# Seven block products for eight in a SwiGLU's gate and up projections, and the down projection moved behind all of them

## The chip, the cores and the metric

The kernel runs on one core of a Trainium2 chip. The metric is the time of one execution in microseconds (us) of the device. An engine's name is that of the profile: PE (TensorE, matmul), DVE (VectorE), ACT (ScalarE), POOL (GpSimd), SP (SyncE, which here issues every DMA).

## The reference

One layer of a hybrid decoder, for 1024 prompt tokens and 8 x 8 sampled ones: a mixer of attention and a state-space group, an output projection, and a SwiGLU feed-forward network (FFN), each between RMS norms. The change concerns the last lines.

```python
mix = jnp.concatenate([o_att.astype(x.dtype), o_ssm], axis=-1) @ w_out
x = x + rmsnorm(mix, g_post_mix)
f = rmsnorm(x, g_pre_ffn)
f = (jax.nn.silu(f @ w_gate) * (f @ w_up)) @ w_down
x = x + rmsnorm(f, g_post_ffn)
return x, new_k, new_v, new_conv, new_ssm
```

D_MODEL is 1024, D_FF is 2816 (22 tiles of 128), all in float32.

## The kernel before

The 1088 tokens stand in three chunks of 384, 384 and 320 columns, features on the partitions. Every float32 product is made of three products in the fp32r format: an operand x is split into xh (a rounding cast, on ACT) and xl = x - xh (on DVE or POOL), and a block of 128x128 weights costs the matmuls wh xh, wh xl and wl xh (`gemm`, L142 to L144). The weights come as raw lots of 128x512 (`load_w`, L119 to L126; 256 KB each): a DMA on SP, the cast on ACT at L125, the subtraction mostly on POOL at L126, with four raw buffers and five for each half.

The order on PE is written out by hand (`weave` gives PE filler work in gaps that the program names in us); on DVE, ACT, POOL and SP a scheduler sets it, and each engine runs its queue in that order.

When a chunk c has its mixer output, `chain(c)` (L1022) makes the norm behind the mixer (pm), the residual, and the norm ahead of the FFN (pf). A norm's sum of squares is added up by PE (`pm1st`), DVE makes the reciprocal root and a diagonal (`pm1d`), and PE broadcasts it (`pm1R`). For chunk 1 these names are pm1 and pf1, and what follows pf1R is f1: eight scalings (L1039), casts and subtractions. While chunk 2 goes through this, PE is filled by `first_up`: gate and up of the first three feature tiles over chunk 0, then 1.

The FFN then runs in eight groups of two or three feature tiles. `up_chunk` makes gate (og) and up (ou) of a tile and a chunk, and splits the result h into th and tl_, which stay in SBUF. Behind the tiles of a group, `down` makes the eight output tiles over the group's features alone and adds them to YP, at L1166 on DVE:

```python
for m in range(8):
    hi, lo = load_w(A["w_d"][m][:, ff0:ff0 + G, :], G, P, "wd%d_%d" % (gi, m))
    for c in range(3):
        down(m, [(hi[:, k, :], lo[:, k, :]) for k in range(G)], c)
```

The last group goes chunk by chunk, with the final norm `fin` (L1187, L1188) of a chunk beside the next one's products, and the outputs go out on SP.

Of the kernel before, what the change touches and what calls it, by code (L numbers as in the profile page):

```python
# [36 lines left out]
def hybrid_layer(ctx, tc, A):  # L37
# [1051 lines left out]
    with pool("chain") as kp:  # L1089

        th, tl_ = [], []

        def first_up():
            while "ch1" not in done:
                yield None
# [240 lines left out]
```

## Time and profile before

| | |
|---|---|
| time, median of 3 runs (lowest to highest) | 1747.24 us (1745.35 to 1752.21) |
| the profiled execution: time, span | 1751.08 us, 1749.3 us |
| mean granted clock of TensorE | 0.973 |
| busy in the span: PE, DVE, ACT, POOL | 1655.3, 881.5, 624.0, 631.4 us |
| DMA over the span | 171.13 MB, 98 GB/s |

Times in the rows are us from the span's start, of one execution. The busy time is a mean over stages: the mixer, up to about 900 us, where all engines work, and the FFN behind it, where PE is nearly always busy and the others are not. A row of the timeline gives start, length, engine, line and instruction (output <- inputs); in brackets stands the time in which its engine was idle just before it, and what ended that.

### The profile page before, as it was taken

The numbers are of one execution on the slowest core, as the hardware profiler recorded it, in microseconds if no ns is written. First come the engines' busy times: TensorE is split into PE (matmuls) and PEld (weight loads), VectorE is DVE, ScalarE is ACT, GpSimd is POOL, SyncE is SP. The second block draws the span as 40 slices with busy tenths as digits, with TensorE's granted clock in tenths as the row PEclk, the third lists the DMA queues.
The fourth block names the chain that finished last, engine by engine and source line by source line (L and its number), as shares of the span: only waits on it lengthen the run. The fifth ranks groups of instructions, "written<-read, shape, count | busy, mean of one in ns | idle before, by whom it ended". The sixth has DMA issues, their size and how long they took to land. (4 is left out here: it accounts for less than half of the span.)

```text
span 1749.3 us, 26692 instructions
## 1 busy us (share of the span) xinstructions
PE 1655.3 (95%) x9959; PEld 1560.4 (89%) x9959; DVE 881.5 (50%) x1917; ACT 624.0 (36%) x1397; POOL 631.4 (36%) x516
## 2 busy tenths in 40 slices
PE   8899999999799989899988999999999999999995
PEld 6899988887777877898988999999999999999995
DVE  6797667763588887346877401211212112121347
ACT  5242344431586676444543232112121121211221
POOL 5262356655554342223555222122222221221432
PEclk9899999999899999999989999999999999999997
DMA  5022564555553341543554111111111111110233
GB/s 185 25 79 99 155 177 141 163 171 194 149 150 93 93 145 58 175 128 105 175 176 143 39 49 41 44 47 38 50 42 50 41 41 46 41 57 22 82 103 102
DMA packets 146441, 171.13 MB, mean 98 GB/s; under 512 B 18120, under 2 KB 106696, under 8 KB 146280
## 3 DMA queue, kind: packets, MB, share of 16 engines
q1 hardware_dynamic: 146312, 169.43, 31.5%
q8 instruction: 78, 1.28, 0.3%
q14 instruction: 51, 0.42, 0.1%
HBM read 135.33 MB, written 36.28 MB: 98 GB/s over the span
## 5 line engine op out<-in xcount | busy, mean ns | idle before, releaser
L1055 DVE TENSOR_TENSOR sg<-sg,ou 128x384 f32<-128x384 f32 (+1 forms) x66 | 35.0, 532 | 393.3 <-PE ou L144 392.7
L1166 DVE TENSOR_TENSOR YP<-YP,od 128x384 f32<-128x384 f32 (+1 forms) x168 | 89.1, 532 | 126.2 <-PE od L144 126.0
L126 POOL TENSOR_TENSOR wg_1l<-wg_1r,wg_1h 128x512 fp32r<-128x512 f32 x20 | 25.9, 1294 | 211.6 <-ACT wg_1h L125 211.6
L1056 ACT CAST ffh<-sg 128x384 fp32r<-128x384 f32 (+1 forms) x66 | 32.6, 495 | 188.6 <-DVE sg L1055 188.3
L126 POOL TENSOR_TENSOR wi_1l<-wi_1r,wi_1h 128x512 fp32r<-128x512 f32 x40 | 56.1, 1403 | 73.9 <-ACT wi_1h L125 70.7
L1051 ACT ACTIVATE sg<-og 128x384 f32<-128x384 f32 (+1 forms) x66 | 31.1, 472 | 131.8 <-PE og L144 125.2
L126 POOL TENSOR_TENSOR wi_0l<-wi_0r,wi_0h 128x512 fp32r<-128x512 f32 x40 | 58.4, 1460 | 30.4 <-ACT wi_0h L125 27.5
L1057 DVE TENSOR_TENSOR ffl<-sg,ffh 128x384 fp32r<-128x384 f32 (+1 forms) x66 | 42.8, 650 | 33.9 <-ACT ffh L1056 33.8
L126 POOL TENSOR_TENSOR woa_1l<-woa_1r,woa_1h 128x512 fp32r<-128x512 f32 x24 | 33.7, 1405 | 64.8 <-ACT woa_1h L125 57.9
L126 POOL TENSOR_TENSOR wos_1l<-wos_1r,wos_1h 128x512 fp32r<-128x512 f32 x24 | 33.9, 1411 | 60.4 <-ACT wos_1h L125 54.8
L142 PE MATMUL ip<-x1h,wi_0h 128*128 128x384 f32 x128 | 48.4, 378 | 6.3 <-DVE cbuf L367 3.0
L380 DVE SCALAR_TENSOR_TENSOR cacc<-cbuf,vec,cacc 128x1112 f32<-128x1112 f32 x36 | 52.3, 1456 | 0.7
L142 PE MATMUL ip<-x0h,wi_0h 128*128 128x384 f32 x128 | 47.5, 371 | 4.5 <-DVE cbuf L367 3.6
L142 PE MATMUL ip<-x0h,wi_1h 128*128 128x384 f32 x128 | 45.6, 357 | 0.0
L144 PE MATMUL ip<-x0h,wi_0l 128*128 128x384 f32 x128 | 43.6, 341 | 1.5 <-POOL wi_0l L126 1.5
L142 PE MATMUL ip<-x1h,wi_1h 128*128 128x384 f32 x128 | 44.8, 350 | 0.0
L126 POOL TENSOR_TENSOR wd_1l<-wd_1r,wd_1h 128x384 fp32r<-128x384 f32 (+1 forms) x7 | 6.8, 973 | 105.2 <-ACT wd_1h L125 105.2
L144 PE MATMUL ip<-x1h,wi_0l 128*128 128x384 f32 x128 | 44.3, 346 | 0.0
L143 PE MATMUL ip<-x1l,wi_0h 128*128 128x384 f32 x128 | 44.2, 345 | 0.0
L143 PE MATMUL ip<-x0l,wi_0h 128*128 128x384 f32 x128 | 43.4, 339 | 0.4 <-DVE x0l L278 0.4
L126 POOL TENSOR_TENSOR wg_0l<-wg_0r,wg_0h 128x512 fp32r<-128x512 f32 x21 | 27.4, 1303 | 45.6 <-ACT wg_0h L125 45.6
L144 PE MATMUL ip<-x0h,wi_1l 128*128 128x384 f32 x128 | 43.8, 342 | 0.0
(840 smaller groups left out, 6136.3 us busy)
## 6 DMA issues: line engine op xcount, KB each, us to landing
wi_0r<-in_w_in SPq DMA_DIRECT2D x40, 256.0 KB
wi_1r<-in_w_in SPq DMA_DIRECT2D x40, 256.0 KB
wos_0r<-in_w_os SPq DMA_DIRECT2D x24, 256.0 KB
wos_1r<-in_w_os SPq DMA_DIRECT2D x24, 256.0 KB
woa_0r<-in_w_oa SPq DMA_DIRECT2D x24, 256.0 KB
woa_1r<-in_w_oa SPq DMA_DIRECT2D x24, 256.0 KB
wg_0r<-in_w_g SPq DMA_DIRECT2D x22, 256.0 KB
wg_1r<-in_w_g SPq DMA_DIRECT2D x22, 256.0 KB
```

What stands on the lines that cost most here:

```text
L126: (eng or g).tensor_sub(lo, raw, fr(hi))
L142: t.matmul(out, lhsT=wh, rhs=xh, start=k == 0, stop=False)
L143: t.matmul(out, lhsT=wh, rhs=xl, start=False, stop=False)
L144: t.matmul(out, lhsT=wl, rhs=xh, start=False, stop=k == n - 1)
L380: v.scalar_tensor_tensor(acc[:, :L], buf[:, k:k + L], vec[:, cw + k:cw + k + 1], acc[:, :L], ALU.mult, ALU.add)
L1051: s.activation(sg, og[:, :n], AF.Silu)
L1055: v.tensor_mul(sg, sg, ou[:, :n])
L1056: s.copy(hi[:, c0:c0 + n], sg)
L1057: v.tensor_sub(lo[:, c0:c0 + n], sg, fr(hi[:, c0:c0 + n]))
L1166: v.tensor_add(YP[m][:, c0:c0 + n], YP[m][:, c0:c0 + n], o[:, :n])
```

## The change

The gate and up projections of two feature tiles (2j and 2j+1) over the two chunks of 384 columns are taken as a product of 2x2 blocks: feature tiles by halves of D_MODEL, times halves of D_MODEL by chunks. In place of eight block products seven are made, by the Winograd form of Strassen's scheme. It needs four sums of weight blocks (S1 to S4, on DVE, for each pair and each of gate and up), four sums of the blocks of the two chunks (T1 to T4, made once in `chain(1)` on DVE and POOL and split into halves like every operand), and sums of the products, on DVE and POOL. B11 and B21 are chunk 0's halves, B22 the second half of chunk 1. A unit (`gu_unit`) is gate or up of one pair: 84 matmuls of 384 columns, and 48 of 320 for chunk 2, whose four block products are made as before. It splits eight lots of weights in place of four.

`first_up` runs the units of pairs 0 and 1 without chunk 2 while that chunk is in `chain(2)`; their chunk 2 part follows with the weights loaded again, and then pairs 2 to 10 whole. The products silu(gate) x up are written to DRAM (h_scr). When all are done, the down projection goes chunk by chunk: `h_load` fetches h in six lots of four feature tiles, two raw buffers (hs) for all, and splits them; then each output tile is made over all 22 feature tiles in one accumulation, its weights loaded for every chunk. `fin` of a chunk stands beside the next chunk's first tile, with four buffers for x2. The groups, YP and the last group's own arrangement go.

```diff
-FFG = [3, 3, 3, 3, 3, 3, 2, 2]
...
+    h_scr = dr.tile([P, NFF, TOK], F32, name="h_scr")
...
-    def chain(c, mt, acc, kp, F):
+
+    ops = {}
+
+    def hilo(name, hi, lo):
+        ops[name] = [(hi[:, k, :], lo[:, k, :]) for k in range(4)]
+
+    def chain(c, mt, acc, kp):
...
-        for k in range(8):
+
+        def scaled(k):
             v.scalar_tensor_tensor(mt[:, k, :], mt[:, k, :], vec[:, V_GPF + k:V_GPF + k + 1], R, ALU.mult, ALU.mult)
-            s.copy(F.hi(k), mt[:, k, :])
-            (g if k % 2 else v).tensor_sub(F.lo(k), mt[:, k, :], fr(F.hi(k)))
-
...
-    def up_chunk(ff, c, wg, wu, hi, lo):
...
+            return mt[:, k, :]
+
+        def split(h, l, k, x, e):
+            s.copy(h[:, k, :], x)
+            e.tensor_sub(l[:, k, :], x, fr(h[:, k, :]))
...
+        elif c == 1:
+
+            m0 = mix[0]
+            t1, t4, t3, t2 = m0[:, 0:4], m0[:, 4:8], mt[:, 0:4], mt[:, 4:8]
+            h, l = Half(c, "B22h"), Half(c, "B22l")
+            slots["B22"] = (h, l)
+            hilo("B22", h.t, l.t)
+            for k in range(4):
+                v.tensor_sub(t1[:, k, :], scaled(k), m0[:, k, :])
+            for k in range(4):
+                split(h.t, l.t, k, scaled(4 + k), g)
+                v.tensor_sub(t3[:, k, :], mt[:, 4 + k, :], mt[:, k, :])
+                v.tensor_sub(t2[:, k, :], mt[:, 4 + k, :], t1[:, k, :])
+                g.tensor_sub(t4[:, k, :], m0[:, 4 + k, :], t2[:, k, :])
+            while "op2" not in done:
+                yield 1.0
+            for name, x, e in (("T2", t2, v), ("T1", t1, v), ("T3", t3, g), ("T4", t4, g)):
+                h, l = Half(c, name + "h"), Half(c, name + "l", at=None if xfree else xl)
+                slots[name] = (h, l)
+                hilo(name, h.t, l.t)
+                for k in range(0, 4, 2):
+                    s.copy(h.t[:, k:k + 2, :], x[:, k:k + 2, :])
+                    e.tensor_sub(l.t[:, k:k + 2, :], x[:, k:k + 2, :], fr(h.t[:, k:k + 2, :]))
...
+    def prod(out, n, w, name, first=False):
+
+        for k in range(4):
+            (wh, wl), (xh, xl) = w[k], ops[name][k]
+            for i, (x, y) in enumerate(((wh, xh), (wh, xl), (wl, xh))):
+                t.matmul(out[:, :n], lhsT=x, rhs=y, start=first and k + i == 0, stop=k == 3 and i == 2,
+                         skip_group_check=not first)
...
+    def gu_unit(gp, src, j, up, sgs, wino, plain):
...
+        if wino:
+            pa, pb, pc = ps("mm", nm + "pa"), ps("s", nm + "pb"), ps("t", nm + "pc")
+            ssum(1, r[21], r[22], False)
+            ssum(2, S[1], r[11], True)
+        w = lot(r[11], 11)
+        if wino:
+            yield from prod(pa, n, w, "B11", True)
+            p1 = st("p1")
+            with tc.high_priority():
+                s.copy(p1, pa[:, :n])
+        if plain:
+            yield from prod(qa, n2, w, "F0", True)
+        if wino:
+            w = lot(S[2], "s2")
+            yield from prod(pb, n, w, "T2", True)
+            u2 = st("u2")
+            with tc.high_priority():
+                v.tensor_add(u2, p1, pb[:, :n])
+            w = lot(S[1], "s1", v)
+            yield from prod(pc, n, w, "T1", True)
+            p5 = st("p5")
+            with tc.high_priority():
+                s.copy(p5, pc[:, :n])
+            ssum(3, r[11], r[21], True)
+            ssum(4, r[12], S[2], True)
+        w = lot(r[12], 12)
+        if wino:
+            yield from prod(pa, n, w, "B21")
+            out(0, 0, 0, v, lambda dst: pa[:, :n])
+        if plain:
+            yield from prod(qa, n2, w, "F1")
+            out(4, 0, 2, v, lambda dst: qa[:, :n2])
+        if wino:
+            w = lot(S[3], "s3")
+            yield from prod(pb, n, w, "T3")
+            u3 = st("u3")
+            with tc.high_priority():
+                v.tensor_add(u3, p1, pb[:, :n])
+            out(1, 1, 1, g, add(g, u3, p5, u3))
+            w = lot(S[4], "s4", v)
+            yield from prod(pc, n, w, "B22")
+            out(2, 0, 1, g, add(v, u2, pc[:, :n], u2))
+        w = lot(r[22], 22)
+        if wino:
+            yield from prod(pb, n, w, "T4")
+            out(3, 1, 0, v, add(v, p1, pb[:, :n], p1))
+        if plain:
+            yield from prod(qb, n2, w, "F1", True)
+            w = lot(r[21], 21)
+            yield from prod(qb, n2, w, "F0")
+            out(5, 1, 2, v, lambda dst: qb[:, :n2])
...
+                while "ch2" not in done:
+                    yield from gu_pair(kp, part[0], plain=False)
+                    part[0] += 1
...
+            for j in range(part[0]):
+                run(gu_pair(gp, j, wino=False))
+            for j in range(part[0], NFF // 2):
+                run(gu_pair(gp, j))
...
+                x = dp.tile([P, 4, n], F32, tag="hs", bufs=2, name="hs%d_%d" % (c, i))
+                dma(x[:, :K], h_scr[:, q:q + K, c0:c0 + n])
+                s.copy(h[:, :K], x[:, :K])
+                v.tensor_sub(l[:, :K], x[:, :K], fr(h[:, :K]))
...
+                hi, lo = load_w(A["w_d"][m][:, q:q + K, :], K, P, "wd%d_%d" % (m, i), eng=v if i % 3 == 2 else g)
+                w = [(hi[:, k, :], lo[:, k, :]) for k in range(K)]
+                for k in range(K):
+                    (wh, wl), (xh, xl) = w[k], H[q + k]
+                    t.matmul(o[:, :n], lhsT=wh, rhs=xh, start=q + k == 0, stop=False)
+                    t.matmul(o[:, :n], lhsT=wh, rhs=xl, start=False, stop=False)
+                    t.matmul(o[:, :n], lhsT=wl, rhs=xh, start=False, stop=q + k == NFF - 1)
...
+            def x2_load(m):
+                x2 = dp.tile([P, n], F32, tag="x2", bufs=4, name="x2_%d" % m)
+                dma(x2, x2_scr[:, m, c0:c0 + n])
...
+        H = h_load(0, range(6), False)
+        for c, (c0, n) in enumerate(CH):
+            Y = dp.tile([P, 8, n], F32, tag="Y", bufs=2, name="Y%d" % c)
+            accs = [sp.tile([P, n], F32, tag="acc", bufs=2, name="acc")]
+            for m in range(8):
...
-            if not last:
-                for m in range(8):
-                    hi, lo = load_w(A["w_d"][m][:, ff0:ff0 + G, :], G, P, "wd%d_%d" % (gi, m))
-                    for c in range(3):
-                        down(m, [(hi[:, k, :], lo[:, k, :]) for k in range(G)], c)
```

On PE, what follows the broadcast pf1R in before is gate and up of tiles 0 and 1 over chunk 0 (f0h, f0l), 24 matmuls each, with chunk 2's norm (pm2st, pm2R) among them. The first use of f1 is the last row, 146 matmuls behind pf1R.

```order
L211 MATMUL pf1R_9718<-pf1d_9671,ones_76 128x128 x3
L142 MATMUL og0_0_9822<-f0h0_8558,wg0_0h_9760 128x384
L143 MATMUL og0_0_9822<-f0l0_8560,wg0_0h_9760 128x384
...
L142 MATMUL ou0_0_9849<-f0h0_8558,wu0_0h_9772 128x384
...
L197 MATMUL pm2st_9874<-ones_76,acc_8923 128x1 x3
L142 MATMUL og1_0_9901<-f0h0_8558,wg1_0h_9784 128x384
...
L142 MATMUL ou1_0_9928<-f0h0_8558,wu1_0h_9796 128x384
...
L211 MATMUL pm2R_9938<-pm2d_9894,ones_76 128x128 x3
...
L142 MATMUL og0_1_10079<-f1h0_9129,wg0_0h_9760 128x384
```

In the changed kernel there stand 12 products on B11 (of chunk 0), then the 12 on T2 and the 12 on T1, both made of chunk 1.

```order
L198 MATMUL pf1R_9718<-pf1d_9671,ones_76 128x128 x3
L1094 MATMUL g0pa_9790<-B11h_9105,g0w11h_9797 128x384
L1094 MATMUL g0pa_9790<-B11l_9106,g0w11h_9797 128x384
...
L1094 MATMUL g0pb_9791<-T2h_9758,g0ws2h_9815 128x384
...
L1094 MATMUL g0pc_9792<-T1h_9764,g0ws1h_9833 128x384
...
L1094 MATMUL g0pa_9790<-B21h_9119,g0w12h_9855 128x384
...
L184 MATMUL pm2st_9871<-ones_76,acc_8923 128x1 x3
L1094 MATMUL g0pb_9791<-T3h_9770,g0ws3h_9897 128x384
...
L1094 MATMUL g0pc_9792<-B22h_9724,g0ws4h_9918 128x384
...
L1094 MATMUL g0pb_9791<-T4h_9776,g0w22h_9937 128x384
...
L198 MATMUL pm2R_9947<-pm2d_9891,ones_76 128x128 x3
```

What moved: the first operand of chunk 1 is needed 12 matmuls behind pf1R, where it was 146, and chunk 2's pm2st stands behind the products on T2 and T1.

On DVE, this is what follows the diagonal pf1d in before: eight scalings of chunk 1 (tile mix1) and four subtractions.

```order
L205 TENSOR_SCALAR pf1d_9671<-cst_74,pf1y_9659 128x128 x3
L1039 SCALAR_TENSOR_TENSOR mix1_7919<-mix1_7919,vec_75,pf1R_9722 128x384
L1020 TENSOR_TENSOR acc_8923<-acc_8923,sq_9715 128x320
L1039 SCALAR_TENSOR_TENSOR mix1_7919<-mix1_7919,vec_75,pf1R_9722 128x384 x2
L1041 TENSOR_TENSOR f1l0_9131<-mix1_7919,f1h0_9129 128x384
L1039 SCALAR_TENSOR_TENSOR mix1_7919<-mix1_7919,vec_75,pf1R_9722 128x384 x3
L1041 TENSOR_TENSOR f1l0_9131<-mix1_7919,f1h0_9129 128x384
L1039 SCALAR_TENSOR_TENSOR mix1_7919<-mix1_7919,vec_75,pf1R_9722 128x384 x2
L1041 TENSOR_TENSOR f1l1_9132<-mix1_7919,f1h1_9130 128x384 x2
```

And in the changed kernel, where mix0 takes t1 and t4, mix1 the scaled chunk, t3 and t2; u0S are sums of up weights of pair 0, g0ws4l the lower half of a gate weight sum:

```order
L192 TENSOR_SCALAR pf1d_9671<-cst_74,pf1y_9659 128x128 x3
L1034 SCALAR_TENSOR_TENSOR mix1_7920<-mix1_7920,vec_75,pf1R_9722 128x384
L1008 TENSOR_TENSOR acc_8923<-acc_8923,sq_9715 128x320
L1113 TENSOR_TENSOR u0S1_10035<-u0r21_10026,u0r22_10028 128x512
L1056 TENSOR_TENSOR mix0_6626<-mix1_7920,mix0_6626 128x384
L1113 TENSOR_TENSOR u0S2_10037<-u0S1_10035,u0r11_10024 128x512
L1086 TENSOR_TENSOR g0ws4l_9919<-g0S4_9853,g0ws4h_9918 128x512
...
L1113 TENSOR_TENSOR u0S4_10095<-u0r12_10030,u0S2_10037 128x512
...
L1070 TENSOR_TENSOR T1l_9765<-mix0_6626,T1h_9764 128x768
...
L1070 TENSOR_TENSOR T2l_9759<-mix1_7920,T2h_9758 128x768
...
L1070 TENSOR_TENSOR T1l_9765<-mix0_6626,T1h_9764 128x768
L1070 TENSOR_TENSOR T2l_9759<-mix1_7920,T2h_9758 128x768
```

What moved: 30 operations stand from pf1R to the last T2l, the sums of chunks and of weights among them.

On SP, at the change from gate and up to down in the changed kernel; g10sg are the products of the last pair, hs0 the lots of h for chunk 0, wd1 the weights of the second output tile:

```order
L1134 DMA h_scr_91<-g10sg_14282 128x384
L1134 DMA h_scr_91<-g10sg_14296 128x320
...
L109 DMA wd1_1r_14762<-in_w_d 128x512
L1134 DMA h_scr_91<-g10sg_14385 128x320
L109 DMA wd1_2r_14780<-in_w_d 128x512
L1279 DMA hs0_0_14602<-h_scr_91 128x4x384
L1279 DMA hs0_1_14608<-h_scr_91 128x4x384
L1304 DMA x2_0_15564<-x2_scr_89 128x384
...
L1279 DMA hs0_2_14614<-h_scr_91 128x4x384
L1279 DMA hs0_3_14620<-h_scr_91 128x4x384
L109 DMA wd1_3r_14798<-in_w_d 128x512
...
L1279 DMA hs0_4_14626<-h_scr_91 128x4x384
```

What is new: the first load of h stands behind the last write of h, and four loads of x2 and some of weights stand among the loads of h.

## Rows read from the trace of the kernel before

**Rows 1.** Windows: stretch, length; busy us of each engine, granted clock, DMA share, GB/s.

```profile
900.00:920.00 20.00, 17.58 (x110) 16.96 (x108) 13.59 (x21) 9.45 (x19) 13.69 (x11) 0.91 0.69 201
920.00:940.00 20.00, 17.59 (x93) 17.11 (x93) 18.30 (x19) 9.20 (x20) 15.95 (x12) 0.91 0.47 148
...
1100.00:1200.00 100.00, 100.00 (x609) 100.00 (x608) 22.48 (x41) 18.97 (x36) 23.68 (x20) 1.00 0.15 46
...
1720.00:1735.00 15.00, 10.92 (x60) 10.20 (x60) 11.61 (x28) 4.20 (x9) 3.75 (x3) 0.78 0.37 133
```

**Rows 2.** Timeline of PE (start, length, instruction): 384-column products, first and thirteenth.

```profile
1149.78 0.35 PE L144 MATMUL og<-f0h,wg_0l 128*128 128x384 f32 x1
...
1151.88 0.34 PE L144 MATMUL og<-f0h,wg_1l 128*128 128x384 f32 x1
```

**Rows 3.** Timeline of PE: 320-column products, first and eighth of a run.

```profile
885.94 0.31 PE L142 MATMUL op<-sh,wos_0h 128*128 128x320 f32 x1
...
886.97 0.31 PE L143 MATMUL op<-sl,wos_0h 128*128 128x320 f32 x1
```

**Rows 4.** Timeline of PE after the first-chunk work, idle time and releaser in brackets.

```profile
921.68 0.46 PE L211 MATMUL pf1R<-pf1d,ones 128*128 128x128 f32 x2 [2.93 <-DVE pf1d L205]
...
943.52 1.62 PE L211 MATMUL pm2R<-pm2d,ones 128*128 128x128 f32 x6 [3.58 <-DVE pm2d L205]
```

**Rows 5.** Timeline of DVE round the broadcast pf1R.

```profile
924.58 0.62 DVE L1039 SCALAR_TENSOR_TENSOR mix<-mix,vec,pf1R 128x384 f32<-128x384 f32 x1 [1.63 <-ACT pf1R L218]
...
928.71 1.65 DVE L1041 TENSOR_TENSOR f1l<-mix,f1h 128x384 fp32r<-128x384 f32 x1
...
935.98 2.93 DVE L1039 SCALAR_TENSOR_TENSOR mix<-mix,vec,pf1R 128x384 f32<-128x384 f32 x2
...
941.05 0.56 DVE L1057 TENSOR_TENSOR ffl<-sg,ffh 128x384 fp32r<-128x384 f32 x1
```

**Rows 6.** Timeline of POOL, the first and last of seven back to back.

```profile
928.33 1.61 POOL L126 TENSOR_TENSOR wx<-wg_0r,wx 128x512 fp32r<-128x512 f32 x1
...
937.16 1.34 POOL L1041 TENSOR_TENSOR f1l<-mix,f1h 128x384 fp32r<-128x384 f32 x1
939.54 1.17 POOL L1041 TENSOR_TENSOR f1l<-mix,f1h 128x384 fp32r<-128x384 f32 x1 [1.04 <-ACT f1h L1040]
```

**Rows 7.** The instructions that read pf0R: min/median/max ns.

```profile
L1039 DVE SCALAR_TENSOR_TENSOR mix<-mix,vec,pf0R x8: 604/611/1646, 863.7 to 873.5; 128x384 f32<-128x384 f32 x8
```

**Rows 8.** Costliest groups (page) and DVE's groups by shape: busy, mean ns.

```profile
L126 POOL TENSOR_TENSOR wg_1l<-wg_1r,wg_1h 128x512 fp32r<-128x512 f32 x20 | 25.9, 1294 | 211.6 <-ACT wg_1h L125 211.6
...
L126 DVE TENSOR_TENSOR wos_0l<-wos_0r,wos_0h 128x512 fp32r<-128x512 f32 x24 | 17.6, 732 | 24.5 <-ACT wos_0h L125 21.7 <-issue 2.8
```

**Rows 9.** The instructions on tile gz: min/median/max ns.

```profile
L967 ACT ACTIVATE gz<-gz x6: 1271/1488/1492, 494.4 to 772.0; 128x1536 f32<-128x1536 f32 x4, 128x1280 f32<-128x1280 f32 x2
...
L968 POOL TENSOR_TENSOR gy<-gy,gz x6: 1557/2384/2620, 496.0 to 773.4; 128x768 f32<-128x768 f32 x4, 128x640 f32<-128x640 f32 x2
...
L971 DVE TENSOR_TENSOR gz<-gz x6: 806/952/959, 504.4 to 778.8; 128x768 f32<-128x768 f32 x4, 128x640 f32<-128x640 f32 x2
```

**Rows 10.** Timelines of SP (issues) and ACT (readers): 256 and 512 KB loads.

```profile
911.93 0.33 SPq L122 DMA_DIRECT2D wg_1r<-in_w_g  x1
...
914.81 0.62 ACT L125 CAST wg_1h<-wg_1r 128x512 fp32r<-128x512 f32 x1 [2.19 <-DMA wg_1r<-in_w_g]
...
277.55 0.36 SPq L540 DMA_DIRECT2D d_1ac<-ac_scr  x1
...
282.39 0.22 ACT L574 ACTIVATE d_1en<-d_1ac 128x8 f32<-128x8 f32 x1 [2.06 <-DMA d_1ac<-ac_scr]
```

**Rows 11.** Timeline of PE: the last group's end.

```profile
1721.18 0.42 PE L142 MATMUL od<-ffh,wx 128*128 128x320 f32 x1 [1.88 <-DVE sg L1055]
...
1724.78 0.39 PE L142 MATMUL od<-ffh,wx 128*128 128x320 f32 x1
...
1729.11 0.31 PE L144 MATMUL od<-ffh,wx 128*128 128x320 f32 x1
```

More of the change, by code (lines that the diff above doesn't have):

```diff
@@ new lines, in hybrid_layer, with split_w @@
+    slots, xl = {}, None
+    def split_w(raw, name, e):
+        hi = wp.tile([P, 4, P], F32R, tag="hi", bufs=5, name=name + "h")
+        lo = wp.tile([P, 4, P], F32R, tag="lo", bufs=5, name=name + "l")
+        s.copy(hi, raw)
+        e.tensor_sub(lo, raw, fr(hi))
+        return [(hi[:, k, :], lo[:, k, :]) for k in range(4)]
+    def prod(out, n, w, name, first=False):
+        for k in range(4):
+            (wh, wl), (xh, xl) = w[k], ops[name][k]
+            for i, (x, y) in enumerate(((wh, xh), (wh, xl), (wl, xh))):
+                t.matmul(out[:, :n], lhsT=x, rhs=y, start=first and k + i == 0, stop=k == 3 and i == 2,
+                         skip_group_check=not first)
+            if k == 1:
+                yield 6 * n / 2400.0
+        yield 6 * n / 2400.0
@@ L1059, in hybrid_layer, with gu_pair @@
+    def gu_pair(gp, j, wino=True, plain=True):
+        sgs = {}
+        for up in range(2):
+            yield from gu_unit(gp, A["w_u" if up else "w_g"], j, up, sgs, wino, plain)
     s_hl, o_hl, mix, acc = [None] * 3, [None] * 3, [None] * 3, [None] * 3
@@ L1074, in ch @@
             yield 1.0
-        fs.append(Split(c, "f%d" % c))
-        yield from chain(c, mix[c], acc[c], kp, fs[c])
+        yield from chain(c, mix[c], acc[c], kp)
         done.add("ch%d" % c)
@@ L1088, in hybrid_layer @@
     done.add("att2")
[L1089 to L1095, printed above, removed]
-            for j, x in (("h", th), ("l", tl_)):
-                x3 = fpool.tile([P, 3, TOK], F32R, tag="F", bufs=3, name="ff%s0" % j)
-                x.extend(x3[:, i, :] for i in range(3))
-            while "op2" not in done:
-                yield None
-            we = [Extra(kp, "s%s2_%d" % (j, q), 1, 2, CH[2][1]) for j in "hl" for q in range(2)]
-            w0 = [(load_w8(A["w_g"][i], P, "wg%d" % i, wq[0]), load_w8(A["w_u"][i], P, "wu%d" % i, wq[1]))
-                  for i, wq in enumerate(((None, None), ((None, kp), (kp, kp)), (we[:2], we[2:])))]
-            for c in range(3):
-                while "ch%d" % c not in done:
-                    yield None
-                for i in range(3):
-                    yield from up_chunk(i, c, w0[i][0], w0[i][1], th[i], tl_[i])
-        f = seq(f, lambda: op(2), first_up)
-        weave(seq(gate(2, kp), ch(0, kp), ch(1, kp), ch(2, kp)), f)
-        run(f)
@@ new lines, in hybrid_layer, with first_up @@
+    with pool("xl") as xl:
+        with pool("chain") as kp:
+            part = [0]
+            def first_up():
+                while "ch1" not in done:
+                    yield None
+                while "ch2" not in done:
+                    yield from gu_pair(kp, part[0], plain=False)
+                    part[0] += 1
+            f = seq(f, lambda: op(2), first_up)
+            weave(seq(gate(2, kp), ch(0, kp), ch(1, kp), ch(2, kp)), f)
+            run(f)
+        with pool("gu") as gp:
+            with tc.issue_after(wdma[0]):
+                for o, a in (("o_ks", "ck_nat"), ("o_vs", "cv_nat")):
+                    dma(A[o][:, 0:P - NT, :], A[a][:, NT:, :])
+            for j in range(part[0]):
+                run(gu_pair(gp, j, wino=False))
+            for j in range(part[0], NFF // 2):
+                run(gu_pair(gp, j))
```

224 lines of the change are left out of this document (107 added, 117 removed).

## The prediction

> **What bounds the kernel now.** I read the windows first. In the FFN TensorE (PE) is busy for the whole of 1100 to 1200 us at full clock, DVE and POOL for under a quarter of it [rows 1]: there time is a count of matmuls times their spacing, and helpers are free. It is otherwise at the seam where the FFN begins (900 to 940): PE is busy 17.6 of 20 us, DVE up to 18.3 and POOL up to 16.0 [rows 1]. There the question is which operand comes last. So I took PE's timeline for the spacing (2.10 us for 12 products of 384 columns, 0.174 each; 1.03 us for 7 of 320, 0.147 each) [rows 2, 3], and then its waits at the seam: 2.93 us for pf1R and 3.58 for pm2R, both on DVE [rows 4], and no wait of 0.4 us or more for the normed chunk f1 itself. That is because 146 matmuls (25 us) stand between pf1R and the first use of f1, as the order of before shows. The last place is the end: PE waits 1.88 us in the last group and then runs at half clock [rows 11].
>
> **What is removed on PE.** The FFN had 3168 products of 384 columns and 1584 of 320. Now a gate or up unit has 7 x 12 = 84 of 384 and 48 of 320, 22 units, and the down projection still has 1056 and 528. That is 2904 and 1584: 264 products fewer, all of 384 columns. 264 x 0.174 = **-46.0 us** [rows 2]. This needs PE to be the bound of each stage, which the rest is about.
>
> In the last group PE's stall goes too, since the up and down products are no longer alternated there: 1.88 us, and 12 products in 3.60 us where 0.147 each would be 1.76 [rows 3, 11]: **-3.7**.
>
> **pf1R, a little later.** Five DVE operations of 128x512 on weights now stand ahead of pf1d (g0S1, g0S2, g0S3, g0S4, g0ws1l). Alone they take 0.73 each [rows 8], 3.7 together, and 1.65 each, 8 together, at the pace of a DVE subtraction beside a busy POOL [rows 5]; a part of it fills waits that were there. **+3.5** (1.5 to 8).
>
> **The sums of chunk 1, the largest cost.** After pf1R the order now has only the 12 products on B11 (2.1 us), and then T2. T2 is a difference of a difference (t1 before t2), and the last to be split on DVE. On DVE 30 operations stand from pf1R to the last T2l: 8 scalings at 0.61 [rows 7], 12 sums of 384 columns at 0.56 [rows 5] and one of 320, 5 of 128x512 at 0.73 [rows 8], 4 of 768 columns at 0.95 [rows 9]: 19.5 us if nothing holds them. In the same stretch POOL has four B22l and four t4 at 1.17 [rows 6], and two of 768 columns, for which 1.9 is scaled from 1557 ns for 640 [rows 9]: 13.2 us. Do the two run beside each other? In before, POOL ran seven subtractions back to back from 928.33 to 938.50 [rows 6] (four of 512 columns at 1.29 alone, three of 384 at 1.17: 8.7 us), and DVE seven operations from 928.71 to 938.91 [rows 5] that alone take 5 x 0.61 + 2 x 0.56 = 4.2 us. So 12.9 us of work took 10.2: an overlap of 1.26, and a DVE scaling went from 0.61 to 1.4 or 1.6 [rows 5, 7]. By this 32.7 / 1.26 = 26 us, and some 2 us for ACT's casts and for u0S4, whose weight is asked for only behind u0S3 (2.9 us from issue to use) [rows 10]. T2 is there 28 us after pf1R, PE has 2.1 us to do: **+26** (18 with DVE's own 20 us; 32 if the two exclude each other, 32.7 us and 1 for a cast).
>
> By the Trainium skill (SBUF — State Buffer, section "SBUF: two separate sides") a DVE operation with two inputs in SBUF and a GpSimd operation that reads SBUF hold one port pair as an exclusive lock. The rows above agree that they slow each other, but the 1.26 says not all of it is serial; by the rule this term would be the upper one, +32.
>
> **Pairs 0 and 1 beside chunk 2.** 336 products of 384 columns, 58.5 us. POOL has 6 weight splits and 2 sums a unit, 6 x 1.29 + 2 x 1.17 = 10.1, 40 in four units, and some 12 of chunk 2; DVE's operations with both inputs in SBUF are near 23. 75 / 1.26 = 60 us, close to PE's 58.5, with pm2R and pf2R to wait for as before (3.58) [rows 4], and half clock behind a long wait as in [rows 11]. **+6** (1 to 12). In the plain part of these pairs that follows, a unit has 48 x 0.147 = 7.1 us of PE against 4 x 1.29 = 5.2 of POOL: **+1** (0 to 6). In the 18 full units PE has 21.7 us against 10 of POOL and about 9 of DVE, so nothing is added.
>
> **From gate and up to down.** Every lot of h now comes back from DRAM, and the load hs0_0 stands behind the last write of h on SP and waits for it. From the last up product: DVE's product 0.55, issue and write about 2.9 (as long as a 256 KB load takes to be used) [rows 10]; the load of 768 KB: 256 KB take 2.88 and 512 KB 4.84 from issue to reader [rows 10], so 6.8 by the same step; ACT's cast 1.5, and DVE's subtraction 1.75 from twice 0.95 [rows 9]. That is 13.5 us to the first lot, 12 if the write lands sooner. There are two buffers, so lots 2 and 3 wait for the subtraction of 0 and 1, and 4 and 5 for those of 2 and 3: about 10 us a turn. The sixth-but-one lot is split at 33 us, and 18 products follow it (3.1 us): the first output tile ends at 34 to 36 us instead of 66 x 0.174 = 11.5. **+22** (14 if loads take 4 us, at the 201 GB/s that one stretch of before shows [rows 1]; 27 if the weight loads of the same queue share it). Behind it a down tile needs 11.5 us of PE and 6 weight splits, 4 of them on POOL (5.2 us): PE bound again, and the changes of chunk, where the x2 loads and outputs queue on SP, **+2** (0 to 6).
>
> **The end.** Now as then some 20 us pass from the last product [rows 11] to the span's end at 1749.3. Four of the eight x2 tiles now load only when the output DMA of their buffer has ended: **+2** (1 to 4).
>
> **Sum.** -46.0 - 3.7 + 3.5 + 26 + 6 + 1 + 22 + 2 + 2 = +12.8. The profiled execution took 1751.08 us (1749.3 of span and 1.8 around it), 3.84 above the median: 1763.9, and 1760 beside the median of 1747.24.
>
> **Rivals.** Faster: DVE is not held by POOL at the seam. For it: the overlap comes from ten microseconds of one execution, with weight splits of POOL that stand elsewhere now. Against it: [rows 5] beside [rows 7]. pf1R costs 1.5 then, T2 18, pairs 0 and 1 1, the plain part 0; with a transition of 18 the sum is -46.0 - 3.7 + 1.5 + 18 + 1 + 18 + 2 + 1 = -8, or 1739, and lower if the loads are quicker too. It decides from the point where T2 is ready under about 22 us after pf1R. No gain and no loss: the first bubble is as computed, but the lots of h come in a stream and cost 10 instead of 22, because loads of one turn fly together and PE works on lots 0 to 3 meanwhile: +1, or 1748. For it speaks that the weights of the first tiles are already there; against it the two buffers. Much slower: POOL and DVE exclude each other. T2 at +32, pf1R +8, pairs 0 and 1 at 75 us instead of 58.5, thus +17, the plain part +3, the transition +24, and 3 and 3 at the chunks and the end: +40, or 1787. For it, the windows of 920 to 940 with 18.3 and 16.0 us of work in 20 [rows 1]; against it, the overlap of 1.26. This is what the page's rule would make of it.
>
> **How the numbers follow.** Forecast 0.40, faster rival 0.25, even 0.22, much slower 0.13. The likeliest case's own bounds, not all low or all high at once, are 1746 to 1774. Leaving out the lower half of the faster rival's spread (about 1725 to 1745) and most of the slow one, 8 in 10 lie in 1736 to 1783. 0.5% or 8.7 us is about what can be told from no change here. Under 1738.5: most of the faster rival's mass that lies low and a little of the even one, 0.20; above 1756: the slow rival and most of the forecast, 0.50; between, 0.30.
>
> **What would show it.** PE should wait some 26 us for DVE's T2l right behind the products of B11, and some 20 us in its first down tile for the splits of hs0_0 to hs0_5; in the full units it should be busy without a gap, 264 products fewer in all. I am wrong if DVE's 30 operations take near 20 us, if the first lot of h is split under 8 us after the last up product, or if PE waits for weight splits in the full units or the down tiles.

## The result: slower by 1.5%, and where it went

The changed kernel takes 1774.53 us (median of 4 runs, 1768.14 to 1777.16) where the kernel before takes 1746.3 on the same chip: a ratio of 1.0155, 95% interval 1.0112 to 1.0198. The profiled execution took 1776.24 us with a span of 1774.5, so 25.2 more than the span before.

The windows of the changed kernel, to be read beside [rows 1] (the same columns). The matmuls that were saved show nowhere here; what shows is PE idle in four places.

```profile
900.00:920.00 20.00, 18.25 (x126) 17.72 (x124) 12.92 (x18) 10.24 (x22) 12.34 (x11) 1.00 0.59 188
920.00:940.00 20.00, 4.38 (x18) 4.09 (x18) 17.28 (x34) 6.05 (x11) 6.79 (x5) 0.62 0.16 52
940.00:960.00 20.00, 7.49 (x23) 6.18 (x24) 14.98 (x11) 5.30 (x8) 16.61 (x11) 0.53 0.00 1
...
1020.00:1040.00 20.00, 12.11 (x65) 11.39 (x64) 4.72 (x9) 4.31 (x9) 10.16 (x9) 0.83 0.50 172
...
1100.00:1200.00 100.00, 100.00 (x609) 100.00 (x608) 38.72 (x59) 31.95 (x58) 48.77 (x39) 1.00 0.25 83
...
1460.00:1480.00 20.00, 8.00 (x26) 7.28 (x27) 6.10 (x5) 6.05 (x7) 1.74 (x3) 0.66 0.81 261
```

From 920 to 960 PE was busy 11.9 of 40 us, where before it was 17.6 in the first 20 alone. The granted clock, 0.62 and 0.53 of full speed, is a mean with half clock in it: PE fell to the lower of its two levels (half clock) while it had nothing to do. From 1100 to 1200 PE is full and the clock 1.00, as before, though DVE is busy for 38.7 us where it was 22.5, and POOL for 48.8 where it was 23.7. The timeline of PE names the waits (these answer to [rows 4, 11]).

```profile
925.26 1.62 PE L198 MATMUL pf1R<-pf1d,ones 128*128 128x128 f32 x6 [6.93 <-DVE pf1d L192]
943.51 0.69 PE L1094 MATMUL g0pb<-T2h,g0ws2h 128*128 128x384 f32 x1 [13.86 <-ACT T2h L1069]
950.27 0.69 PE L1094 MATMUL g0pb<-T2l,g0ws2h 128*128 128x384 f32 x1 [6.08 <-DVE T2l L1070]
954.17 0.69 PE L1094 MATMUL g0pb<-T2h,g0ws2h 128*128 128x384 f32 x1 [1.94 <-ACT T2h L1069]
955.85 0.69 PE L1094 MATMUL g0pb<-T2l,g0ws2h 128*128 128x384 f32 x1 [0.99 <-DVE T2l L1070]
988.15 0.69 PE L1094 MATMUL u0pb<-T4h,u0w22h 128*128 128x384 f32 x1 [4.34 <-DVE u0u L1182]
1033.59 0.64 PE L1094 MATMUL g0qa<-f2h,g0w11h 128*128 128x320 f32 x1 [7.44 <-ACT g0w11h L1085]
1470.31 0.69 PE L1294 MATMUL od<-Hh,wd_0h 128*128 128x384 f32 x1 [10.43 <-ACT Hh L1280]
1489.22 0.69 PE L1295 MATMUL od<-Hl,wd_4h 128*128 128x384 f32 x1 [1.35 <-DVE Hl L1281]
1581.99 0.83 PE L184 MATMUL fin0st<-ones,acc 128*128 128x1 f32 x6 [2.35 <-POOL acc L1008]
```

I read stages from the first and last start of each matmul group on PE. Bare matmuls (0.174 and 0.147 us each) against time taken: pairs 0 and 1 over two chunks, 58.5 against 99.5 us; their plain part for chunk 2, 28.2 against 40.4; pairs 2 to 10, 390.1 against 393.3; the down projection, 261.4 against 293.8; then 21 us to the end. In the kernel before, the start of the FFN (gate and up of the first three tiles) took some 82.4 against 71.3, the rest lost 10.4 in all, and the end took 20.0.

| term, us | forecast | profile |
|---|---|---|
| 264 matmuls of 384 columns | -46.0 | -46.0 |
| losses of before behind its start (last group) | -3.7 | -10.4 |
| start of the FFN later (pf1R, and the mixer) | +3.5 | +2.8 |
| wait for T2, and pairs 0 and 1 beside chunk 2 | +26 and +6 | +29.9 (41.0 less 11.1) |
| plain part | +1 | +12.2 |
| full units | 0 | +3.2 |
| first down tile (35.4 for 11.5 us) | +22 | +23.9 |
| changes of chunk | +2 | +8.5 |
| the end | +2 | +1.0 |
| sum | +12.8 | +25.1 (the spans differ by 25.2) |

The +2.8 does not measure what pf1R costs: 2.6 of it is the mixer, which ended that much later in this profile than in the one before. From pm1R to the first product took 41.8 us before, 42.1 here and 44.8 in the second profile of the changed kernel (experiment 11), so pf1R's own part is 0.2 to 2.9.

One caution on totals. The mixer, whose operations the change leaves as they are, ended (start of pm1R) at 881.9 us in the profile before and anywhere from 870.0 to 884.5 in the others, the changed kernel itself at 884.5 and, in a second profile, at 873.7. So a median of four runs carries some microseconds of the mixer's chance, and I judge experiments by both: the ratio to the kernel before, and stage lengths, which repeat (the changed kernel again: 99.2, 40.5, 392.3, 293.5).

### The profile page after: what moved, and what is told of

It is laid out like the page before. It is cut to its first block, busy times and chain, and to the rows that moved or that the text cites. A ratio compares the mean times of both kernels' runs of the same rounds, so it can differ in the third digit from the quotient of the medians.

```text
span 1774.5 us, 27385 instructions
## 1 busy us (share of the span) xinstructions
PE 1628.1 (92%) x9695; PEld 1528.4 (86%) x9695; DVE 977.9 (55%) x1959; ACT 747.5 (42%) x1581; POOL 840.4 (47%) x660
## 4 chain that ended last, share of the span: by engine, by line
PE 57%; DVE 11%; DMA 5%; issue 4%; POOL 3%; ACT 3%; SPq 1%; POOLq 0%; DVEq 0%; ACTq 0%
PE od L1295 4%; PE od L1296 4%; PE od L1294 4%; PE ip L129 2%; PE op L129 2%; PE op L130 2%; PE op L131 2%; PE ip L130 2%; PE ip L131 2%; DMA hs<-h_scr 1%; DMA xr<-in_xT 1%; DVE a_0S L735 1%; ACT a_1S L730 1%; DMA g0r<-in_w_g 1%; DMA x<-x_scr 1%
## 5 line engine op out<-in xcount | busy, mean ns | idle before, releaser
L113 POOL TENSOR_TENSOR woa_1l<-woa_1r,woa_1h 128x512 fp32r<-128x512 f32 x24 | 33.7, 1403 | 67.2 <-ACT woa_1h L112 63.0
L113 DVE TENSOR_TENSOR wd_2l<-wd_2r,wd_2h 128x512 fp32r<-128x512 f32 x24 | 20.3, 847 | 71.7 <-ACT wd_2h L112 68.9
L113 POOL TENSOR_TENSOR wd_3l<-wd_3r,wd_3h 128x512 fp32r<-128x512 f32 x24 | 32.6, 1356 | 56.2 <-ACT wd_3h L112 56.2
L113 POOL TENSOR_TENSOR wd_0l<-wd_0r,wd_0h 128x512 fp32r<-128x512 f32 x24 | 32.5, 1353 | 50.8 <-ACT wd_0h L112 49.2
L113 DVE TENSOR_TENSOR wd_5l<-wd_5r,wd_5h 128x256 fp32r<-128x256 f32 x24 | 16.7, 695 | 53.2 <-ACT wd_5h L112 53.2
L131 PE MATMUL ip<-x1h,wi_0l 128*128 128x384 f32 x128 | 44.8, 350 | 0.0
L130 PE MATMUL ip<-x0l,wi_1h 128*128 128x384 f32 x128 | 43.7, 341 | 0.0
L131 PE MATMUL ip<-x1h,wi_1l 128*128 128x384 f32 x128 | 43.3, 338 | 0.0
L130 PE MATMUL ip<-x1l,wi_1h 128*128 128x384 f32 x128 | 43.3, 338 | 0.0
L129 PE MATMUL ip<-x2h,wi_0h 128*128 128x320 f32 x128 | 43.1, 337 | 0.1
```

The costliest lines, as they stand in the source:

```text
L113: (eng or g).tensor_sub(lo, raw, fr(hi))
L129: t.matmul(out, lhsT=wh, rhs=xh, start=k == 0, stop=False)
L130: t.matmul(out, lhsT=wh, rhs=xl, start=False, stop=False)
L131: t.matmul(out, lhsT=wl, rhs=xh, start=False, stop=k == n - 1)
```

## The experiments

My theory: three waits made by order and place (T2 right behind pf1R; the plain part's weights; the way of h through DRAM) eat the 46 us. The rivals say that DVE, POOL or the queues bound those stages, so that taking one wait away only moves it.

**1. Without the T sums.** The sums and splits are left out; products take other operands.

```diff
+for name, x in (("T2", "B11"), ("T1", "B11"), ("T3", "B21"), ("T4", "B21")):
+    ops[name] = ops[x]
```

> Leaves out the four sums T1 to T4 of the chunks and their splits: the products on T2 and T1 take the halves of B11, those on T3 and T4 those of B21, so the products are not those of the reference; the matmuls, weight sums and all else stay. My theory: the wait for T2 right behind pf1R is what the FFN's start lost, 41 us above the bare matmuls of pairs 0 and 1 where before lost 11 in its own start. Then PE runs on behind pf1R, that loss falls to 10 to 14, and the time to 1745 to 1750. Rival: the weight sums and eight splits a unit on DVE and POOL beside chunk 2 bound this stage whatever T does; then PE waits for weight splits instead, the loss stays at 25 to 30, and the time is near 1761.

1747.43 us, ratio 0.9995 (0.9979 to 1.001). Pairs 0 and 1 took 78.5 us, so the loss fell from 41 to 20, between the two forecasts (10 to 14, and 25 to 30): half is the T sums, half is not. The time did land where it was expected, but with help: the stages behind pf1R give 22 of its 27 us, and the mixer ended 6 us earlier in this profile. What stayed was a wait for u0u (a sum of products, made on DVE) and others of 1 to 2 us (PE's timeline of this kernel):

```profile
963.05 0.69 PE L1083 MATMUL u0pb<-B21h,u0w22h 128*128 128x384 f32 x1 [4.68 <-DVE u0u L1171]
```

**2. The sums that T2 needs first on DVE.**

```diff
+with tc.high_priority():
+    for k in range(4):
+        v.tensor_sub(t1[:, k, :], scaled(k), m0[:, k, :])
...
+        if k % 2:
+            tsplit("T2", t2, v, k - 1)
```

> The same work, but on DVE the sums that T2 needs and T2's split stand ahead of T1's, of the weight sums of the next unit and of g0ws4l, and POOL makes t4, T3 and T4 behind them. My theory: T2 is late by its place in DVE's queue. T2 should be split 16 to 19 us behind pf1R instead of 29, PE idles 10 us less there, part of it is given back in later waits of unit g0, so the time falls by 6 to 11, to 1764 to 1769. Rival: DVE and POOL together are the bound (some 33 us of operations), so that what T2 gains T3 or T4 lose within the same unit: a fall of 0 to 3.

1769.91 us, ratio 1.0119 (1.0102 to 1.0136); pairs 0 and 1 took 97.4 us. T2 was complete 27.3 us behind the start of pf1R (25.6 behind its end, not 16 to 19): the rival was right here. The order changed only in part, since both splits of T1 still stand ahead of the last T2l. DVE's timeline of this kernel shows what else holds T2: DVE has almost only this chunk's work in its queue, but once POOL runs (from 926.6 us on) most operations take two to four times their length (experiment 5 has them alone).

```profile
933.07 1.75 DVE L1066 TENSOR_TENSOR T2l<-mix,T2h 128x768 fp32r<-128x768 f32 x1
934.74 2.63 DVE L1073 TENSOR_TENSOR mix<-mix 128x384 f32<-128x384 f32 x2
...
939.84 4.22 DVE L1066 TENSOR_TENSOR T1l<-mix,T1h 128x768 fp32r<-128x768 f32 x2
943.99 1.74 DVE L1066 TENSOR_TENSOR T2l<-mix,T2h 128x768 fp32r<-128x768 f32 x1
```

POOL's timeline of the same kernel and the same stretch, with the split of B22 and POOL's half of T:

```profile
933.97 2.98 POOL L1039 TENSOR_TENSOR B22l<-mix,B22h 128x384 fp32r<-128x384 f32 x2
936.92 2.11 POOL L1066 TENSOR_TENSOR T4l<-mix,T4h 128x768 fp32r<-128x768 f32 x1
...
940.74 2.51 POOL L1066 TENSOR_TENSOR T3l<-mix,T3h 128x768 fp32r<-128x768 f32 x1
```

**3. The plain part's weights ahead of the writes of h.** 

```diff
                     e.tensor_mul(sg, sg, put(None))
-                    dma(h_scr[:, 2 * j + m, c0:c0 + nc_], sg)
+            if up:
+                dma(h_scr[:, 2 * j + m, c0:c0 + nc_], sgs[i])
```

> The writes of h lose their raised priority, so that in SP's queue the four gate weights of the plain part of pair 0 stand ahead of the four writes of g1sg. My theory: the plain part lost 12 us because its weights were asked for only behind writes that waited for the last products of pair 1. Then the 7.4 us wait ahead of g0qa falls to under 2 and the time by 7 to 10, to 1765 to 1768. Rival: the plain part is bound by POOL's splits or by the raw buffers, which come free late: a fall of 0 to 3.

1768.99 us, ratio 1.0121 (1.0094 to 1.0147), but the plain part took 39.6 us: nothing was won there, and the lower median is within the mixer's chance. The wait ahead of g0qa went, and one of 6.55 came ahead of u0qa, for the gate result g0sg. PE's timeline of this kernel:

```profile
1042.92 0.63 PE L1094 MATMUL u0qa<-f2h,u0w11h 128*128 128x320 f32 x1 [6.55 <-ACT g0sg L1129]
```

ACT's timeline of the same kernel says what g0sg itself waited for, the writes of g1sg, now late on SP, whose space it takes:

```profile
1042.43 0.44 ACT L1129 ACTIVATE g0sg<-g0qa 128x320 f32<-128x320 f32 x1 [2.36 <-DMA h_scr<-g1sg]
```

**4. h by lots.** 

```diff
-    h_scr = dr.tile([P, NFF, TOK], F32, name="h_scr")
+    h_scr = [dr.tile([P, 4, TOK], F32, name="h_scr%d" % i) for i in range(6)]
...
+        hp = ctx.enter_context(pool("hsp"))
...
-                x = dp.tile([P, 4, n], F32, tag="hs", bufs=2, name="hs%d_%d" % (c, i))
-                dma(x[:, :K], h_scr[:, q:q + K, c0:c0 + n])
+                x = hp.tile([P, 4, n], F32, tag="hs", bufs=2, name="hs%d_%d" % (c, i))
+                dma(x[:, :K], h_scr[i][:, :K, c0:c0 + n])
```

> h goes to six tensors in DRAM, one for each lot of four feature tiles, and the two raw buffers hs are taken from a pool of their own, so the loads of the first lots need not wait for the last write of h nor for the end of the stage; x2 has three buffers instead of four. My theory: of the 24 us that the first down tile lost, the wait for the last write and the first load are 10 us and the turns of the two buffers the rest. With lots 0 and 1 loaded early and 2 and 3 following sooner, 12 to 18 us come back, 1757 to 1763. Rival: the loads themselves and SP's queue set the pace of the lots, so only the first wait goes: a fall of 3 to 6.

1759.84 us, ratio 1.006 (1.0039 to 1.0081); the down projection took 276.1 us instead of 293.8, as forecast. Two things are changed together, the tensors and the space of the raw buffers, and no run takes them apart. In the first tile one wait of PE is left, for the last lot, which does depend on the last write (PE's timeline of this kernel):

```profile
1474.05 0.69 PE L1296 MATMUL od<-Hh,wd_5h 128*128 128x384 f32 x1 [3.20 <-ACT Hh L1282]
```

**5. The sums on DVE alone.** Experiment 2, with `v` for `g` in the split of B22, in t4, and in T3 and T4, which stand last.

> The same work, but every sum and split of chunk 1 is made by DVE, T2's and T1's ahead of T3's and T4's and of the weight sums; POOL has none of it. My theory after the second experiment: the sums were not late by their place in the queue alone, but because POOL's subtractions stretch DVE's from 0.5 to 1.3 and more; all of it on DVE alone is some 23 us, and T2 needs 17 of them. T2 should be complete 19 to 21 us behind the start of pf1R instead of 30.6 (and 27.3 with POOL taking part), and the time falls by 7 to 11, to 1764 to 1768. Rival: DVE's queue is the bound with or without POOL; the operations keep their stretched length because POOL splits weights meanwhile; a fall of 0 to 4.

1766.51 us, ratio 1.0105 (1.008 to 1.0129). T2 was complete 18.7 us behind the start of pf1R. DVE's timeline, the same operations as above:

```profile
932.34 0.95 DVE L1066 TENSOR_TENSOR T2l<-mix,T2h 128x768 fp32r<-128x768 f32 x1
933.21 0.55 DVE L1074 TENSOR_TENSOR mix<-mix,mix 128x384 f32<-128x384 f32 x1
...
936.82 0.94 DVE L1066 TENSOR_TENSOR T3l<-mix,T3h 128x768 fp32r<-128x768 f32 x1
937.69 0.95 DVE L1066 TENSOR_TENSOR T2l<-mix,T2h 128x768 fp32r<-128x768 f32 x1
```

0.95 where it was 1.75, with POOL idle: T2 was late by the pace that POOL leaves DVE. Of the 11.8 us won there, 6.6 are left in the stage (92.9 us); 4.0 went into a wait for pm2R, which DVE now comes to later (PE's timeline of this kernel):

```profile
956.59 0.76 PE L198 MATMUL pm2R<-pm2d,ones 128*128 128x128 f32 x2 [4.00 <-DVE pm2d L192]
```

**6. The plain part, both waits.** Experiment 3, and the chunk 2 gate result in the pool of `stage`, whose space is free.

```diff
-sg = gp.tile([P, nc_], F32, tag="sg2" if c == 2 else "sg", ...
+sg = stage(nc_, nm + "sg") if c == 2 else gp.tile([P, nc_], F32, tag="sg", ...
```

> The third experiment's order (weights ahead of the writes of g1sg), and the gate results of chunk 2 go to a buffer of another pool, so that they don't wait for the writes of g1sg to end. My theory: the plain part lost 12 us by two waits in a row, for weights behind the writes of h, and, when those went ahead, for the space that g1sg held until it was written. With both gone the plain part takes 29 to 32 us instead of 40.4 and the time falls by 8 to 11, to 1763 to 1767. Rival: raw buffers and POOL's four splits a unit set the pace; the part stays at 37 us or more and the time within 3 of the changed kernel.

1760.49 us, ratio 1.0074 (1.0049 to 1.0099). The plain part took 30.9 us, 9.5 less, as forecast; the median fell by more than that, which I put down to the mixer's chance (pm1R at 875.3), without a run that shows it.

**7. Eight products.** `gu_unit` makes eight block products for chunks 0 and 1, with lots 11, 12, 22 and 21 alone; `chain(1)` splits B12 and B22 as chunk 0's halves are split.

> Undoes the one half of the change: chunks 0 and 1 take eight block products a unit as chunk 2 does, with four weight splits a unit and no sums; h in DRAM and the down projection chunk by chunk stay. My theory: 264 matmuls come back, 46 us, and the FFN's start loses 8 to 12 us instead of 41, because B12 is there some 8 us behind pf1R and no sum stands on DVE; the full units lose nothing. 1774.5 + 46 - 30 - 3 = 1787, 1780 to 1795; so the seven products would be worth some 13 us as they stand, and the way of h and the plain part cost the rest. Rival: the start's loss comes from chunk 2's norm and the weights, not from the sums; then 25 us stay and the time is 1800 or more.

1776.2 us, ratio 1.016 (1.0136 to 1.0184). Pairs 0 and 1 took 74.0 us for 66.9 of products, pairs 2 to 10 took 428.2 (no loss), the rest as in the changed kernel. By stages that is 11.3 us more than the changed kernel, close to the 13 expected; the median shows only 1.7 more and lies under the forecast of 1780 to 1795. In the profiled run the mixer ended at 874.0; beside the changed kernel's second profile, with 873.7 (experiment 11), the span is 9.2 longer. Whether the mixer was as early in the other three runs no trace shows. So, by the stages, seven products win 34.9 us in pairs 2 to 10 and pay 25.5 back in the start.

**8. All together.** Experiments 4, 5 and 6, and the squares of the down projection's output added on DVE.

> The sums on DVE alone, the plain part with weights first and the other buffer, h by lots with its own buffers, and the squares of the down projection's output added by DVE instead of POOL. My theory: the three waits lie at three places and their prices add up: -9, -9, -15 and -2 from 1774.5 give 1739.5, 1735 to 1746, under the kernel before. Rival: what one edit gives back is lost in the next wait of PE's queue; the sum is -15 to -22 and the time 1753 to 1760.

1740.81 us, ratio 0.9953 (0.9934 to 0.9972): faster than the kernel before. The stages took 94.4, 30.1, 393.9 and 276.1 us: the prices add up (32.5 us less than in the changed kernel, where 6.6, 9.5 and 17.7 make 33.8), since the waits lie at different places.

**9 and 10. Eight products until T is there.** Pairs 0 and 1 by eight, B12 split beside the sums, which then are first used by pair 2; in the tenth with experiments 4 and 6 and the squares of the eighth.

```diff
 def gu_pair(gp, j, wino=True, plain=True):
+    if not plain:
+        sgs = {}
+        for up in range(2):
+            yield from gu_unit8(gp, A["w_u" if up else "w_g"], j, up, sgs)
+        return
```

> The changed kernel with pairs 0 and 1 made of eight products over chunks 0 and 1 (B12 is split for them in space that their sums no longer take), the T sums made meanwhile and first used by pair 2. Nothing else is changed. My theory: the start's loss of 41 us is the wait for operands of chunk 1 and for sums of weights and products between DVE and POOL; without them the stage of pairs 0 and 1 takes 66.9 us of products and 8 to 14 of loss, 75 to 81 instead of 99.5, so the time falls by 18 to 24 though 48 products are added. Rival: the T sums, now beside chunk 2's norm on DVE's queue, hold up pm2R and pf2R; the stage takes 85 or more and the gain is under 14.

> The same with the three other edits of the eighth experiment (plain part's weights ahead of the writes and its own buffer, h by lots, squares on DVE). My theory: the prices add up again; beside the eighth experiment's 94 us of its start this one takes 75 to 81, so 13 to 19 us under its 1740.8: 1722 to 1728, 0.985 to 0.99 of the kernel before. Rival: pm2R and pf2R are held up by the sums and the plain part behind them starts later: 1735 to 1741.

Ninth: 1756.5 us, ratio 1.0062 (1.0042 to 1.0082); tenth: 1733.97 us, 0.9919 (0.9903 to 0.9936). Both gain on the changed kernel, and the tenth on the kernel before, but their first stage took 92.9 and 91.9 us, not 75 to 81. Of the ninth's 18 us in the median the stages show 10; its mixer ended at 870.0. The rival was right about the place: in both, DVE makes the sums ahead of pm2's diagonal. The tenth kernel's PE:

```profile
954.74 1.62 PE L198 MATMUL pm2R<-pm2d,ones 128*128 128x128 f32 x6 [13.29 <-DVE pm2d L192]
```

**11. The changed kernel once more.**

> The changed kernel once more, unchanged, on the chip of these runs. The mixer ahead of pm1R, which no experiment touches, ended at 874 to 884 us in the profiles so far. If that is chance of a run, this one ends it elsewhere in that range while its stages behind pf1R take the same 99.5, 40, 393 and 294 us; if it belongs to the kernel, pm1R is at 884 again, 1 at most to either side.

1774.28 us, ratio 1.0148 (1.0121 to 1.0174). Its profile has pm1R at 873.7 and a span of 1765.3, with the stages that the section on the result gives: chance of an execution, not of the kernel.

**12. The sums behind chunk 2's norm.** 

```diff
-v.tensor_sub(t1[:, k, :], mt[:, k, :], m0[:, k, :])
+v.scalar_tensor_tensor(t1[:, k, :], mt[:, k, :], one, m0[:, k, :], ALU.mult, ALU.subtract)
...
+v.tensor_scalar(one, R2[:, 0:1], 0.0, 1.0, op0=ALU.mult, op1=ALU.add)
+late[0](one)
```

> The tenth kernel with the T sums of chunk 1 moved on DVE's queue from ahead of chunk 2's pm2 norm to behind it (t1 and t3 take a factor of one that is made from pm2R, so that they can't stand earlier). My theory after the ninth and tenth: the start still lost 25 us because pm2R waited 13 us for DVE, which had the sums first; the loss goes with the queue's order. The wait for pm2R falls from 13.3 to 3 to 6 us, some of the sums' 14 us come out again ahead of pf2R, and the stage of pairs 0 and 1 takes 78 to 85 us instead of 92: the time falls by 6 to 12, to 1722 to 1728. Rival: DVE's work in this stage, not its order, is the bound; the wait moves to pf2R whole and the time stays within 3 of 1734.

1726.41 us, ratio 0.989 (0.9862 to 0.9919), the best of all. This interval still touches the tenth's (0.9903 to 0.9936); the first stage, 85.6 us instead of 91.9, shows the gain, though less than the 78 to 85 expected. The wait for pm2R is gone, and 8.3 us came out one step later, at the sum of squares for pf2 (PE's timeline of this kernel):

```profile
960.44 0.56 PE L184 MATMUL pf2st<-ones,acc 128*128 128x1 f32 x2 [4.05 <-DVE acc L1008]
965.21 2.29 PE L184 MATMUL pf2st<-ones,acc 128*128 128x1 f32 x10 [4.21 <-POOL acc L1008]
```

## Why the prediction was right, and where it was not

It said slower, 1760 us in a range of 1736 to 1783; 1774.5 was measured. The outline holds: the matmuls saved are worth about what was said (experiment 7: 34.9 us in pairs 2 to 10, where 216 x 0.174 is 37.6), and two new waits with what hangs on them cost more than that. The time alone would not show it. 1774.5 lies just past the upper end of the likeliest case's own bounds (1746 to 1774), a little nearer to the 1787 of the much slower rival than to 1760. The moment of T2 and the stages have to decide: pairs 0 and 1 lost 29.9 us more than the start of before, where the forecast had 32 and that rival 49.

T2 came when it was said. The last T2l of the changed kernel ended 28.9 us behind the end of pf1R, where 28 was forecast and 33.7 in the much slower rival, and PE's waits for it add up to 22.9 us, where some 26 were said. DVE's timeline there shows the stretched lengths that the overlap of 1.26 stood for: a T2l of 768 columns 1.75 and 1.65, a difference of 384 columns 2.15.

```profile
948.47 1.75 DVE L1070 TENSOR_TENSOR T2l<-mix,T2h 128x768 fp32r<-128x768 f32 x1
951.11 2.15 DVE L1060 TENSOR_TENSOR mix<-mix,mix 128x384 f32<-128x384 f32 x1 [0.89 <-POOL B22l L1039]
953.18 0.94 DVE L1070 TENSOR_TENSOR T1l<-mix,T1h 128x768 fp32r<-128x768 f32 x1
954.15 1.65 DVE L1070 TENSOR_TENSOR T2l<-mix,T2h 128x768 fp32r<-128x768 f32 x1
```

POOL's timeline of the same kernel and the same stretch:

```profile
948.15 1.25 POOL L1061 TENSOR_TENSOR mix<-mix,mix 128x384 f32<-128x384 f32 x1 [0.49 <-DVE mix L1060]
951.03 1.81 POOL L1070 TENSOR_TENSOR T3l<-mix,T3h 128x768 fp32r<-128x768 f32 x1
953.34 1.65 POOL L1061 TENSOR_TENSOR mix<-mix,mix 128x384 f32<-128x384 f32 x1 [0.49 <-DVE mix L1060]
```

The two together show that the reason was not an overlap. Each of the three stretched DVE operations ends a fixed time behind the POOL instruction that was running when it started: 0.82 us (948.47), 0.42 (951.11) and 0.81 (954.15). So do all 23 stretched ones of 384 and 768 columns in the changed kernel between 850 and 1000 us, and those of the kernel before ([rows 5, 6]: f1l ends at 930.36, POOL's split at 929.94). That is nearly what such operations need with POOL idle, where they follow each other in 0.47 and 0.87 us. So DVE ran behind POOL's instruction and hardly beside it, as the much slower rival had it. Its 33.7 was too high because the lengths added up were: with DVE idle, a subtraction of 384 columns takes POOL 1.01 us (wd_1l of the kernel before, at 1108.88), not 1.17, and DVE starts its next operation 0.08 before the end of the last. With these, DVE's 30 operations and the 11 of POOL that stand there come to some 30 us (an estimate), and they took 28.4. So that 28 was met is in part luck: lengths too long were divided by an overlap that is hardly there.

The Trainium skill (SBUF — State Buffer, section "SBUF: two separate sides") lets one of the two engines wait out the other's whole instruction. The trace agrees, by the 0.42 and 0.82 us above.

Experiments 2 and 5 tell the place in DVE's queue and POOL's share apart. Counted from the start of pf1R, T2 was complete at 30.5 us in the changed kernel, at 27.3 with the order alone changed, and at 18.7 with POOL's part taken away as well: 3.3 us are the order's, 8.5 POOL's. In these 8.5 is a wait of 0.89, since a difference for T2 is written over what POOL's B22l reads (the bracket at 951.11 shows one such wait). What the T sums cost in all is 21 us by experiment 1, where 26 was forecast; the other 9 of the 29.9 stand against the +6 for pairs 0 and 1.

The first down tile came as worked out, too: the first two results of the down projection, copied by ACT, lie 11.6 us apart, and the first ended 35.4 us behind the last up product (34 to 36 was said), with 16.6 us of PE's waits for the splits in it. SP's waits of the changed kernel from 1460 to 1470 us show the first load of h held until the last write had landed (us in total, times, longest):

```profile
SPq L1279 <- DMA h_scr<-g10sg: 1.5, 1, 1.5
```

With the loads freed of the last write and given buffers of their own, 17.7 us of the stage go (experiment 4; the shares of the two are not shown). SP's queue of the changed kernel at the change from up to down:

```profile
1460.48 0.38 SPq L1134 DMA_DIRECT2D h_scr<-g10sg  x1
1461.80 0.33 SPq L109 DMA_DIRECT2D wd_2r<-in_w_d  x1
1463.86 0.92 SPq L1279 DMA_DIRECT2D hs<-h_scr  x2
1464.83 2.40 SPq L1304 DMA_DIRECT2D x<-x_scr  x4
1472.07 2.28 SPq L1279 DMA_DIRECT2D hs<-h_scr  x2
```

Beside the overlap, the step that failed is the plain part, "a unit has 48 x 0.147 = 7.1 us of PE against 4 x 1.29 = 5.2 of POOL: +1". It measured +12.2, twice the 6 that was its upper bound. I compared engines and left out the queue that feeds them, though the prediction had followed that queue for h. SP asked for nothing between 1001 and 1023 us, then wrote g1sg, and only then asked for the weights (its queue in the changed kernel):

```profile
1001.17 0.80 SPq L1250 DMA_DIRECT2D out_o_ks<-in_ck_nat  x1
1022.96 5.68 SPq L1134 DMA_DIRECT2D h_scr<-g1sg  x4
1028.73 1.86 SPq L1108 DMA_DIRECT2D g0r<-in_w_g  x4
```

Experiments 3 and 6 show two causes in a row, the order on SP and the space of g1sg; with one removed the other takes its place, with both 9.5 us come back.

Smaller misses: the changes of chunk, 8.5 us instead of 2, among them the wait for POOL's squares (2.35); the full units, 3.2 instead of 0; and the losses of before, of which I had only counted the last group (10.4, not 3.7), which worked the other way. Of the start's loss that is not T (20 us in experiment 1) some 13 go with the sums of weights and of products and the half clock behind their waits: experiment 7, which has neither sum, lost 7.1 in that stage at a mean granted clock of 0.99, against 0.90 in experiment 1. How the 13 divide is not shown.

## What to carry to other kernels

When an algorithm saves matmuls by sums of operands, price the moment at which the first sum is needed, not its work: here nine pairs paid for it easily and the first two did not, and eight products for those two, with seven behind, beat the changed kernel, and with the other waits taken away as well the kernel before too (experiments 9, 10 and 12). A tensor in DRAM is one thing to wait for as long as it is one tensor: cut it at the grain at which it is read back. When a wait goes and its stage keeps its length, or gives back less than the wait, read the same engine's next wait: it has the next cause's name on it (experiments 3, 10 and 12).

## What was not expected of the hardware

How far POOL slows DVE goes by the POOL instruction it meets, and not by an overlap: a subtraction of 384 columns takes DVE 0.55 us with POOL idle, 1.65 where it meets one of POOL's weight splits of 512 columns [rows 5, 6], and 2.15 where it meets a split of 768 (951.11 above); one of 768 columns takes 0.95 alone and 1.65 to 1.75 in T2l's rows above. With POOL's part moved to DVE, the two engines' work was done sooner by one alone: the last split of this chunk ended 26.8 us behind the start of pf1R in experiment 5, 29.6 in experiment 2.
